# Hybrid decoder step on one core: head order of small products, per-pair recurrent decode outputs, and what each output projection pass waits for

## The chip, the cores and the metric

The kernel runs on one core of a Trainium2 chip. The metric is the device time of one execution in microseconds (us). A core has a matrix engine (PE, TensorE), three elementwise engines (DVE or VectorE, ACT or ScalarE, POOL or GpSimd), a queue that issues most transfers (SP), on-chip memory (SBUF), and the matrix engine's result memory (PSUM). Each engine runs its own instructions in a fixed order, so one that waits also holds up all that stand behind it on the same engine.

## The reference

One step of a decoder layer on 256 new prompt positions and 8 decode sequences with one new token each, 264 columns in all, in float32:

```
x = x + 0.5 * swiglu(rmsnorm(x), ffn1)
proj = rmsnorm(x) @ w_in                      # q, k, v and the recurrent columns
o_att  = windowed attention with sinks (16 query heads, 4 key/value heads)
o_rwkv = recurrent mixing (16 heads of 64), below
x = x + concat(o_att, o_rwkv) @ w_out
x = x + 0.5 * swiglu(rmsnorm(x), ffn2);  y = rmsnorm(x)
```

The recurrence, per head, with a 64x64 state S (value rows, key columns), is

```
sa = S @ (-kk)
S  = S * w + sa (x) (kk*a) + v (x) k        # w, a per key column; (x) is an outer product
y  = S @ r
out = (groupnorm(y) * ln_w + ln_b + sum(r*k*r_k) * v) * g
```

For the prompt it runs over 256 positions (done here in four chunks of 64). For decode it is a single step from a given state, for 8 sequences and 16 heads. The new states are outputs too. For one step the output can also be written without the new state, which is what the change uses: y = S0 @ (w*r) - (S0 @ kk) * (b.r) + v * (k.r), with b = kk*a and S0 the old state.

## The kernel before

Activations lie transposed: 128 features on the partitions, 264 columns (256 prompt positions, then 8 decode tokens). Every large product is split in two float32r parts: the weights arrive by SP in chunks of up to 128x512 (`raw`), ACT rounds them (`hi`), DVE subtracts (`lo`), and PE does three products for each 128x128 block (`gemm`, L125). These products write `acc` tiles, of which there are three; all other products write `m` tiles, of which there are five.

The step has four parts: the first feed-forward, the mixing, the output projection (with the mixing in one function, `mixing_body`), and the second feed-forward. In the mixing, 38 tiles of w_in are multiplied one after the other (`win`, L329). The rest of the mixing is written as Python generators in a list `tasks`; after each weight chunk `tick` (L76) advances every task by one step, so that small work is emitted between pieces of the large products. The order on each engine is then fixed when the program is built, by a scheduler that places the emitted instructions in a simulated timeline; the code's order and the blocks under high priority are only its input.

The tasks are: `prep` (L356), one for each pair of recurrent heads (8 pairs), which makes the decays, keys and the Gram matrices of the pair; `chain` (L470), one for each batch of two pairs (4 batches), which solves the triangular systems on DVE through DRAM scratch and carries the state over the chunks; `attend` (L713), one for each of eight query tiles of two heads; `dec_attend` (L754), decode attention; and `dec_rwkv` (L635), the decode recurrence of all pairs in sixteen slices of the state, on DVE and POOL. Each slice loads its piece of S (`ld<-in_st`), makes sa with a product on POOL and a sum on DVE (L656), updates S, stores it (`out_wkvs`, L663), and makes y with another product and sum (`yr`, L665). `dec_out` (L669) then transposes y, norms it and adds the affine terms (`yd`).

`XD` collects the eight decode columns of kk, decay, b, v, k and r; `XR` is its transposed copy. Loads of tasks share a ring `ld` of six buffers (L296). Query tiles `q` have a ring of three (L844), so the eviction of a fourth waits until the first attention task has used its own.

The output projection (L872) runs in three passes over the 16 input tiles: tiles 0 to 5 (recurrent pairs 0 to 5), tiles 8 to 15 (attention), tiles 6 and 7 (recurrent pairs 6 and 7). Ahead of each pass `need` (L863) lists the tasks that it drains; before the first pass it also drains `dec_rwkv` and `dec_out`. `drain` (L81) advances all tasks until those listed are done. `split` (L855) then rounds the inputs in two parts, for recurrent tiles after putting the decode columns `yd*gdec` in.

Two heads of a pair lie on partitions 0 to 63 and 64 to 127, `HALF[h]`. Products of 64 rows for one head use one half of the PE rows. Most loops over such products run all of head 0, then all of head 1 (L420, L442, L516, L528, L542, L553, L720); some already alternate (L448, L584).

Of the kernel before, what the change touches and what calls it, by code (L numbers as in the profile page):

```python
# [45 lines left out]
def body(tc, I, O):  # L46
# [34 lines left out]
    def drain(only):  # L81
        while any(g in only for g in tasks):
            tick()
# [9 lines left out]
    with ExitStack() as ctx:  # L93
# [195 lines left out]
        def mixing_body(mx, n2, n3):  # L289
# [14 lines left out]
            XD = fix((P, 6, NPAIR, NB), "XD")  # L304
            gdec = fix((P, NPAIR, NB), "gdec")
            bvdec = fix((P, NPAIR, NB), "bvdec")
# [12 lines left out]
            XR = fix((P, 6, 64), "XR")  # L319
            yr = fix((P, 64), "yr")  # L320
            sa = fix((P, 64), "sa")
            yd = fix((P, 64), "yd")
# [33 lines left out]
            def prep(p, bt, k, xrr, xk, xv):  # L356
# [61 lines left out]
                G.tensor_copy(bvdec[:, p, :], bv[:, NP:T])  # L418
                yield
                for h in range(2):  # L420
                    r = HALF[h]
                    gp = mp()
                    for c in range(4):
                        mm(gp[:, c * P:(c + 1) * P], BK[r, c, h:h + 2, :], KR[r, 0:2, c, :])
                    gm = ring((P, 4, P), "gm", NGM)
                    bt.Gm[k][h] = gm
                    tt(V, gm, gp.rearrange("p (c t) -> p c t", c=4), bc(msk.unsqueeze(1), (P, 4, P)), ALU.mult)
# [14 lines left out]
                for h in range(2):  # L442
                    r, o = HALF[h], HALF[1 - h]
                    for c in range(4):
                        mm(gv[r, c * 64:c * 64 + 64], bt.Gm[k][h][o, c, 0:64], bt.UV[o, c, k, r])
# [24 lines left out]
            def chain(bt):  # L470
# [45 lines left out]
                for h in range(2):  # L516
                    for k in range(n):
                        for c in range(4):
# [9 lines left out]
                for h in range(2):  # L528
                    r = slice(h * 64 + 32, h * 64 + 64)
                    for j in range(4 * n):  # L530
                        mm(ps[h * 64:h * 64 + 32, j * 32:j * 32 + 32], zs[r, j, :], TT[r, j, 32:64])
# [9 lines left out]
                for k in range(n):  # L541
                    for h in range(2):  # L542
                        r = HALF[h]
                        for c in range(4):
# [8 lines left out]
                for k in range(n):  # L553
                    for h in range(2):
                        r = HALF[h]
                        for c in range(1, 4):
                            x = (c - 1) * P
                            mm(pbs[k][r, x:x + 64], W[r, k, c - 1, :], bt.BT[k][c // 2][r, c % 2, r])
                            mm(pbs[k][r, x + 64:x + P], W[r, k, c - 1, :], bt.Gm[k][h][r, c, 64:128])
# [40 lines left out]
                for k in range(n):  # L600
                    A.copy(Ys[k][:, :NP], pY[:, k * NP:(k + 1) * NP])
                for k in range(n):
# [3 lines left out]
                gs = [gnorm(Ys[k][:, :NP], NP, Ys[k][:, :NP]) for k in range(n)]  # L606
# [4 lines left out]
                for k in range(n):  # L611
# [3 lines left out]
                    stt(o[:, :NP], o[:, :NP], vc(VLW + p), bt.bv[k][:, :NP], ALU.mult, ALU.add)  # L615
                    stt(o[:, :NP], o[:, :NP], vc(VLB + p), gp[:, :NP], ALU.add, ALU.mult)
                    A.copy(gdec[:, p, :], gp[:, NP:T])
# [3 lines left out]
            def gnorm(y, n, outp):  # L621
                yp = mp()
                mm(yp[:, :n], cm, y)
                sq = tmp()
                act(sq[:, :n], yp[:, :n], AF.Square)
                yield from pause(PW[3])
                vp = mp()
                mm(vp[:, :n], bo, sq[:, :n])
                r = tmp()
                act(r[:, :n], vp[:, :n], AF.Sqrt, scale=1.0 / 64, bias=eps[:, 1:2])  # L630
                V.reciprocal(r[:, :n], r[:, :n])  # L631
                tt(V, outp, yp[:, :n], r[:, :n], ALU.mult)
                yield

            def dec_rwkv(last):  # L635
                while last.left:
                    yield
                ps = mp()
                for i in range(6):
# [3 lines left out]
                A.copy(XR, ps[:, :384].rearrange("p (c t) -> p c t", c=6))  # L643
# [7 lines left out]
                for k in range(64 // n):  # L651
# [3 lines left out]
                    tt(G, t1, S, bj(0), ALU.mult)  # L655
                    V.tensor_reduce(out=sa[:, r], in_=t1, op=ALU.add, axis=AX.X)  # L656
# [6 lines left out]
                    SP.dma_start(O["wkvs"][:, r, :], S)  # L663
                    tt(G, t2, S, bj(5), ALU.mult)
                    V.tensor_reduce(out=yr[:, r], in_=t2, op=ALU.add, axis=AX.X)  # L665
                    if k % 2:
                        yield

            def dec_out():  # L669
                ps = mp()  # L670
                for h in range(2):
                    r = HALF[h]
                    mm(ps[r, 0:64], yr[r, :], ident[r, r])
                A.copy(yd, ps[:, 0:64])
                yield
                yield from gnorm(yd, 64, yd)
# [342 lines left out]
```

## Time and profile before

| | us |
|---|---|
| median of 3 runs | 2114.09 |
| lowest and highest | 2106.59, 2114.15 |
| the profiled execution | 2113.38 |
| its span, first to last instruction | 2111.5 |

The profile is of the one profiled execution. PE, DVE, ACT and POOL are the engines, and PEld is the weight load of PE, which overlaps it. L and a number is a line of the kernel; a helper that emits every operation has one line for all (L72 is every product, L56 most elementwise operations on two tensors), so groups are read by the names of tiles: `acc<-s,hi` is a product that reads tiles `s` and `hi` and writes `acc`. A float32 product is recorded as two MATMULs (two passes), a float32r product as one. In a group, `x` is the count of records, then busy time and mean duration, then the idle time just before them and who ended it. PEclk is the TensorE clock that was granted, as a share of full speed. In a view by windows each row is a stretch of the span, with the busy time and count of each engine, the clock, the share of DMA time and GB/s.

### The profile page before, as it was taken

The page shows a single profiled execution, that of the slowest core. Times are in us where ns is not written, and L with a number is a line of the kernel's source. Part 1 is how long each engine was busy: PE and PEld are TensorE (multiplying, and loading weights), DVE is VectorE, ACT ScalarE, POOL GpSimd, SP SyncE. Part 2 cuts the span into 40 slices and gives each one's busy share as a digit, 9 for nine tenths or more (in the row PEclk, how much of TensorE's full clock was granted, in tenths as well). Part 3 has the DMA queues.
Part 4 walks back from the last instruction along what each step waited for, and adds up shares of the span by engine and source line. Part 5 has one row for each costly group of instructions (what it writes and reads, how often), then busy time and mean ns, then how long its engine had stood idle before and what let it go on. Part 6 is the DMA issues. An engine that isn't in the chain of part 4 may idle for free.

```text
span 2111.5 us, 45349 instructions
## 1 busy us (share of the span) xinstructions
PE 2045.6 (97%) x16966; PEld 1997.4 (95%) x16966; DVE 1327.7 (63%) x2631; ACT 1061.5 (50%) x2078; POOL 311.1 (15%) x404
## 2 busy tenths in 40 slices
PE   8999999999999999999986899999999999999997
PEld 8999999999999999999975589899999999999997
DVE  5765555556555577876888646756555565655555
ACT  5644444444444576756532444644444444444445
POOL 0301011020101122201044110210110101011012
PEclk9999999999999999999996679999999999999998
DMA  6555565656555574544442155556555565555554
GB/s 221 176 175 187 175 206 170 211 181 181 182 177 185 178 233 150 150 118 129 122 139 79 38 147 183 165 181 181 181 178 184 177 185 182 178 184 175 187 177 139
DMA packets 227535, 356.29 MB, mean 169 GB/s; under 512 B 42177, under 2 KB 83153, under 8 KB 227281
## 3 DMA queue, kind: packets, MB, share of 16 engines
q1 hardware_dynamic: 221616, 344.72, 52.4%
q10 hardware_dynamic: 5696, 8.66, 1.1%
q8 instruction: 133, 2.18, 0.4%
q14 instruction: 90, 0.73, 0.1%
HBM read 345.15 MB, written 10.21 MB: 168 GB/s over the span
## 4 chain that ended last, share of the span: by engine, by line
PE 92%; DVE 4%; DMA 1%; ACT 1%; issue 1%; SPq 0%; DVEq 0%; ACTq 0%
PE acc L72 83%; PE m L72 9%; DVE lo L56 1%; DMA sb<-Xt 0%; DVE ld L56 0%; DMA raw<-in_gu 0%; DVE t L56 0%; DVE st L56 0%; ACT L66 0%; DVE y L56 0%; DVE t L631 0%; DVE s L59 0%; ACT t L66 0%; PE m L737 0%; DVE Xt L56 0%
## 5 line engine op out<-in xcount | busy, mean ns | idle before, releaser
L72 PE MATMUL acc<-s,hi 128*128 128x264 f32 x7072 | 1315.1, 286 | 13.3 <-ACT hi L121 7.7
L56 DVE TENSOR_TENSOR lo<-raw,hi 128x512 fp32r<-128x512 f32 (+2 forms) x1304 | 876.6, 676 | 606.4 <-ACT hi L121 583.2
L121 ACT CAST hi<-raw 128x512 fp32r<-128x512 f32 (+2 forms) x1304 | 780.4, 602 | 879.8 <-PE acc L72 802.2
L72 PEld LDWEIGHTS acc<-s,hi 128*128 128x128 f32 x7072 | 1107.0, 190 | 21.4 <-ACT hi L121 7.7
L72 PE MATMUL acc<-s,lo 128*128 128x264 f32 x3536 | 1013.4, 287 | 2.0 <-DVE lo L56 1.9
L72 PEld LDWEIGHTS acc<-s,lo 128*128 128x128 f32 x3536 | 669.1, 189 | 5.4 <-DVE lo L56 3.9
L72 PE MATMUL acc<-t,hi 128*128 128x264 f32 x2752 | 503.0, 285 | 1.6 <-ACT t L250 1.6
L72 PEld LDWEIGHTS acc<-t,hi 128*128 128x128 f32 x2752 | 426.5, 189 | 1.9 <-ACT t L250 1.8
L72 PE MATMUL acc<-t,lo 128*128 128x264 f32 x1376 | 388.8, 285 | 0.0
L56 POOL TENSOR_TENSOR t<-t,t 128x264 f32<-128x264 f32 (+1 forms) x146 | 156.8, 1074 | 1197.3 <-ACT hi L121 897.5
L72 PEld LDWEIGHTS acc<-t,lo 128*128 128x128 f32 x1376 | 258.4, 188 | 0.0
L56 DVE TENSOR_TENSOR t<-acc,t 128x264 f32<-128x264 f32 x164 | 70.9, 432 | 36.9 <-PE acc L72 36.5
L56 POOL TENSOR_TENSOR s<-s,s 128x264 f32<-128x264 f32 (+1 forms) x56 | 48.7, 871 | 199.0 <-ACT s L66 180.3
L66 ACT ACT_TABLE_LOAD x42 | 53.9, 1283 | 2.9 <-PEq L1011 1.2
L59 DVE SCALAR_TENSOR_TENSOR s<-acc,s 128x264 f32<-128x264 f32 x96 | 40.6, 427 | 16.6 <-PE acc L72 16.1
L59 DVE SCALAR_TENSOR_TENSOR x<-acc,x 128x264 f32<-128x264 f32 x96 | 40.6, 427 | 10.0 <-PE acc L72 9.5
L66 ACT ACTIVATE t<-t 128x264 f32<-128x264 f32 x94 | 40.0, 425 | 3.4 <-DVE t L56 1.9
L250 ACT CAST t<-t 128x264 fp32r<-128x264 f32 x86 | 35.5, 412 | 3.6 <-POOL t L56 2.1
L56 DVE TENSOR_TENSOR st<-X,Xt 128x60 f32<-128x60 f32 (+10 forms) x120 | 28.1, 234 | 12.9 <-DMA Xt<-sa 6.6
L342 POOL COPY shc<-pj 128x9 f32<-128x9 f32 x26 | 20.0, 768 | 85.9 <-DVE pj L56 85.9
L72 PE MATMUL m<-s,hi 128*128 128x264 f32 x160 | 30.3, 289 | 0.3 <-ACT hi L121 0.3
L66 ACT ACTIVATE t<-t,sta 128x256 f32<-128x256 f32 (+2 forms) x33 | 14.7, 446 | 28.3 <-DVE sta L63 27.1
(210 smaller groups left out, 1095.9 us busy)
## 6 DMA issues: line engine op xcount, KB each, us to landing
raw<-in_gu SPq DMA_DIRECT2D x688, 256.0 KB, 3.2
raw<-in_dn SPq DMA_DIRECT2D x224, 256.0 KB, 2.7
raw<-in_win SPq DMA_DIRECT2D x152, 256.0 KB, 3.3
raw<-in_dn SPq DMA_DIRECT2D x160, 192.0 KB, 2.7
raw<-in_wout SPq DMA_DIRECT2D x48, 256.0 KB, 3.0
raw<-in_wout SPq DMA_DIRECT2D x32, 128.0 KB, 2.4
xsp<-x ACTq DMA_DIRECT2D x16, 132.0 KB, 3.5
s<-xsp SPq DMA_DIRECT2D x16, 132.0 KB, 3.0
```

The lines of the kernel that those rows point to most:

```text
L56: return e.tensor_tensor(out=out, in0=a, in1=b, op=op)
L59: return V.scalar_tensor_tensor(out=out, in0=a, scalar=s, in1=b, op0=op0, op1=op1)
L66: return A.activation(out=out, in_=in_, func=f, **k)
L72: TE.matmul(out, lhsT, rhs, start=start, stop=stop, **k)
L121: A.copy(hi[:, :w], raw[:, :w])
L250: A.copy(hi, u)
L342: G.tensor_copy(shc[:, t, :], pj[:, NP:NP + NB + 1])
```

## The change

Five things:

1. Loops over products of half height take the two heads in turn, in `prep` (Gram matrices and the product `gv`), in `chain` (four loops) and in `attend`. For the Gram matrices and the attention scores both heads' PSUM tiles are taken at once.
2. `prep` computes the decode output of its pair. It loads the pair's old state, transposed (`sT`, a new input layout of the same values, two loads of 128x256), and multiplies it on PE with the eight tokens' kk and w*r: sixteen products of 64x64 by 2 columns, and one of 128x128 by 16 columns that sums b.r and k.r over each head. One ACT copy and three small DVE operations finish y, in `XD[:, 7]`.
3. `chain` copies these eight columns beside its 256 prompt columns, and the group norm (`gnorm`) and the affine terms run on 264 columns. `dec_out`, `bvdec`, `gdec`, `yd`, `yr` and `sa` go.
4. `dec_rwkv` becomes `dec_state`: it only updates the states, with sa taken from `XD[:, 0]`. Of its former operations for each slice the two sums on DVE and two of the four products on POOL go. It is spawned when the first projection pass begins, and drained after the last.
5. Before a pass that uses no attention tile, `drain` holds the attention tasks back; `split` is emitted at high priority.

```diff
-    def tick():
+    def tick(hold=()):
         for g in list(tasks):
-            if next(g, tasks) is tasks:
+            if g not in hold and next(g, tasks) is tasks:
                 tasks.remove(g)
...
-                for i, src in ((0, kk), (2, b), (3, xv), (4, kx), (5, xrr)):
+                for i, src in ((6, kk), (2, b), (3, xv), (4, kx), (5, xrr)):
                     G.tensor_copy(XD[:, i, p, :], src[:, NP:T])
+                dq = ring((P, 2, NB), "dq", 3)
+                tt(G, XD[:, 7, p, :], XD[:, 1, p, :], XD[:, 5, p, :], ALU.mult)
+                tt(G, dq, XD[:, 2:5:2, p, :], bc(XD[:, 5:6, p, :], (P, 2, NB)), ALU.mult)
+                st = [load(I["sT"][p, :, 4 * i:4 * i + 4], (P, 4, 64)) for i in range(2)]
...
-                G.tensor_copy(bvdec[:, p, :], bv[:, NP:T])
-                yield
-                for h in range(2):
-                    r = HALF[h]
-                    gp = mp()
-                    for c in range(4):
-                        mm(gp[:, c * P:(c + 1) * P], BK[r, c, h:h + 2, :], KR[r, 0:2, c, :])
+                dps = mp()
+                for i in range(NB):
+                    for h in range(2):
+                        r = HALF[h]
+                        mm(dps[r, 2 * i:2 * i + 2], st[i // 4][r, i % 4, :], XD[r, 6:8, p, i])
+                mm(dps[:, 16:32], bo, dq.rearrange("p s b -> p (s b)"))
+                dv = dps[:, 0:16].rearrange("p (b s) -> p s b", s=2)
+                A.copy(XD[:, 0, p, :], dv[:, 0])
+                tt(V, dq, dps[:, 16:32].rearrange("p (s b) -> p s b", s=2), XD[:, 0:4:3, p, :], ALU.mult)
+                tt(V, dq[:, 0], dv[:, 1], dq[:, 0], ALU.subtract)
+                tt(V, XD[:, 7, p, :], dq[:, 0], dq[:, 1], ALU.add)
+                yield
+                gps = [mp(), mp()]
+                for c in range(4):
+                    for h in range(2):
+                        r = HALF[h]
+                        mm(gps[h][:, c * P:(c + 1) * P], BK[r, c, h:h + 2, :], KR[r, 0:2, c, :])
...
                 for k in range(n):
-                    for h in range(2):
-                        r = HALF[h]
-                        for c in range(4):
+                    for c in range(4):
+                        for h in range(2):
+                            r = HALF[h]
                             mm(wus[k][r, c * P:c * P + P], TT[r, k * 4 + c, :], bt.KR[k][r, 0:3:2, c, :])
...
                     A.copy(Ys[k][:, :NP], pY[:, k * NP:(k + 1) * NP])
+                    A.copy(Ys[k][:, NP:T], XD[:, 7, bt.p0 + k, :])
...
                     S = load(I["st"][:, r, :], shp)
                     t1, t2 = tmp(shp), tmp(shp)
-                    tt(G, t1, S, bj(0), ALU.mult)
-                    V.tensor_reduce(out=sa[:, r], in_=t1, op=ALU.add, axis=AX.X)
+                    tt(G, t1, bc(XR[:, 3, r].unsqueeze(2), shp), bj(4), ALU.mult)
                     tt(V, S, S, bj(1), ALU.mult)
-                    yield
-                    tt(V, t2, bc(sa[:, r].unsqueeze(2), shp), bj(2), ALU.mult)
+                    tt(V, t2, bc(XR[:, 0, r].unsqueeze(2), shp), bj(2), ALU.mult)
                     tt(V, S, S, t2, ALU.subtract)
-                    tt(G, t1, bc(XR[:, 3, r].unsqueeze(2), shp), bj(4), ALU.mult)
                     tt(G, S, S, t1, ALU.add)
                     SP.dma_start(O["wkvs"][:, r, :], S)
-                    tt(G, t2, S, bj(5), ALU.mult)
-                    V.tensor_reduce(out=yr[:, r], in_=t2, op=ALU.add, axis=AX.X)
-                    if k % 2:
-                        yield
+                    yield
...
                 for h in range(2):
                     r = HALF[h]
+                    mm(spp[h][:, 0:256], q[r, P:NP], kT[p][r, 0:NP])
+                for h in range(2):
+                    r = HALF[h]
+                    mm(spp[h][:, 256:384], q[r, 0:P], kT[p][r, 0:P])
...
-                drain(need(ks))
-                for k in ks:
-                    split(k)
+                drain(need(ks), att if max(ks) < 8 else ())
+                if pi == 0:
+                    dst = spawn(dec_state())
+                with tc.high_priority():
+                    for k in ks:
+                        split(k)
...
+            drain([dst])
             return xr
```

More of the change, by code (lines that the diff above doesn't have):

```diff
@@ L515, in chain @@
                 ps = mp()
-                for h in range(2):
-                    for k in range(n):
-                        for c in range(4):
+                for k in range(n):
+                    for c in range(4):
+                        for h in range(2):
                             j = k * 4 + c
@@ L527, in chain @@
                 ps = mp()
-                for h in range(2):
-                    r = slice(h * 64 + 32, h * 64 + 64)
-                    for j in range(4 * n):
+                for j in range(4 * n):
+                    for h in range(2):
+                        r = slice(h * 64 + 32, h * 64 + 64)
                         mm(ps[h * 64:h * 64 + 32, j * 32:j * 32 + 32], zs[r, j, :], TT[r, j, 32:64])
@@ L541, in chain @@
                 for k in range(n):
-                    for h in range(2):
-                        r = HALF[h]
-                        for c in range(4):
+                    for c in range(4):
+                        for h in range(2):
+                            r = HALF[h]
                             mm(wus[k][r, c * P:c * P + P], TT[r, k * 4 + c, :], bt.KR[k][r, 0:3:2, c, :])
@@ L553, in chain @@
                 for k in range(n):
[L554 to L557, printed above, removed]
+                    for c in range(1, 4):
+                        x = (c - 1) * P
+                        for h in range(2):
+                            r = HALF[h]
                             mm(pbs[k][r, x:x + 64], W[r, k, c - 1, :], bt.BT[k][c // 2][r, c % 2, r])
+                        for h in range(2):
+                            r = HALF[h]
                             mm(pbs[k][r, x + 64:x + P], W[r, k, c - 1, :], bt.Gm[k][h][r, c, 64:128])
@@ L605, in chain @@
                 gps = []
-                gs = [gnorm(Ys[k][:, :NP], NP, Ys[k][:, :NP]) for k in range(n)]
+                gs = [gnorm(Ys[k]) for k in range(n)]
                 for _ in range(PW[3] + 1):
```

76 lines of the change are left out of this document (26 added, 50 removed).

## The prediction

> **What bounds the kernel now.** I read the page first: the span, the granted clock, the chain that ended last.
>
> ```profile
> span 2111.5 us, 45349 instructions
> ...
> PEclk9999999999999999999996679999999999999998
> ...
> PE 92%; DVE 4%; DMA 1%; ACT 1%; issue 1%; SPq 0%; DVEq 0%; ACTq 0%
> ```
>
> The chain runs on PE nearly everywhere. Only slices 22 to 24 of 40 have a lower clock: the end of the mixing. The changed program leaves both feed-forwards in their order, so I cut the mixing and the projection into stages by the view of windows. A (790 to 1048) is most of the w_in tiles with the pairs; B ends where the sixth query tile is evicted; C ends at the first product of the projection; D is its three passes. Two short windows of C and the first pass of D follow.
>
> ```profile
> core 0: us, PE busy (x) PEld busy (x) DVE busy (x) ACT busy (x) POOL busy (x), PEclk, DMA share, GB/s
> 790.00:1048.00 258.00, 256.71 (x2379) 242.09 (x2379) 196.12 (x508) 167.60 (x383) 42.21 (x90) 0.99 0.47 134
> 1048.00:1154.00 106.00, 79.38 (x752) 71.18 (x752) 88.41 (x246) 35.05 (x91) 41.85 (x55) 0.83 0.41 117
> 1154.00:1231.00 77.00, 65.80 (x375) 47.27 (x374) 48.73 (x169) 31.83 (x101) 16.22 (x31) 0.59 0.21 63
> 1231.00:1330.00 99.00, 98.70 (x844) 96.56 (x845) 60.41 (x125) 45.90 (x96) 7.29 (x15) 0.97 0.52 162
> ```
> ```profile
> 1160.00:1170.00 10.00, 10.00 (x74) 8.50 (x73) 3.99 (x10) 1.49 (x5) 2.14 (x3) 0.50 0.08 26
> 1210.00:1220.00 10.00, 10.00 (x33) 6.54 (x33) 4.41 (x22) 4.92 (x21) 0.00 (x0) 0.50 0.61 173
> 1231.00:1266.00 35.00, 34.70 (x320) 32.56 (x321) 16.05 (x42) 13.92 (x32) 2.54 (x10) 0.92 0.51 148
> ```
>
> A and D are PE from end to end. In B PE idles 26.6 us while DVE works 88.4 of 106. In C PE works 65.8 of 77, at a clock of 0.59, on attention and the last batch, with no large product beside it. What PE waited for in B and C, from the view of waits:
>
> ```profile
> PE m L72 <- DVE TN L513: 10.8, 1, 10.8
> PE m L737 <- DVE t L63: 9.4, 3, 7.5
> PE m L72 <- ACT s L601: 4.9, 1, 4.9
> PE m L72 <- ACT t L66: 3.7, 2, 2.1
> PE acc L72 <- DVE q L59: 3.6, 1, 3.6
> ```
>
> The three that end on DVE make 23.8 us. DVE's groups in B say what it did; these five are the decode recurrence, 12 of its 16 slices:
>
> ```profile
> L56 DVE TENSOR_TENSOR ld<-ld,t 128x256 f32<-128x256 f32 x12 | 6.6, 548 | 0.0
> L56 DVE TENSOR_TENSOR ld<-ld,XR 128x256 f32<-128x256 f32 x12 | 6.3, 523 | 0.0
> L56 DVE TENSOR_TENSOR t<-sa,XR 128x256 f32<-128x256 f32 x12 | 6.0, 496 | 0.0
> L656 DVE TENSOR_REDUCE sa<-t 128x4 f32<-128x256 f32 x12 | 4.9, 409 | 3.4 <-POOL t L56 3.4
> L665 DVE TENSOR_REDUCE yr<-t 128x4 f32<-128x256 f32 x12 | 4.9, 408 | 0.0
> ```
>
> Together 28.7 us of B.
>
> **The change, part by part. Stage A: price of the small products.** From the timeline of PE (start, duration, count of records, two to a product):
>
> ```profile
> 949.93 1.10 PE L72 MATMUL m<-C,bk 64*128 64x64 f32 x8
> 1052.87 1.71 PE L72 MATMUL m<-kr,bk 64*128 64x128 f32 x16
> 1057.00 0.96 PE L72 MATMUL m<-uv,gm 64*64 64x64 f32 x16
> 1057.90 1.11 PE L72 MATMUL m<-C,bk 64*128 64x64 f32 x16
> 1058.93 0.92 PE L72 MATMUL m<-C,XD 64*64 64x64 f32 x24
> 1067.81 2.56 PE L72 MATMUL m<-kr,TT 64*64 64x128 f32 x32
> ```
>
> The first row is four products of one head in a row (the scheduler had parted the heads there), the fourth is eight in alternation: the same time for twice the work. So alternation halves this form. C,XD alternates already and takes 38 ns a record; uv,gm, of its size in head order, takes 60.
> - Gram matrices (kr,bk), halved: 1.71 to 0.86 us, 7 pairs in A: -6.0. Ends: -6.0 and 0.
> - gv (uv,gm) at 38 ns: 0.96 to 0.61 us, 7 pairs: -2.5.
> - W and U (kr,TT), halved: 1.28 us off each batch, two in A: -2.6.
> - The two 32x32 loops and the one behind W I leave at nothing.
> - Added: 16 products of 64x64 by 2 columns, 32 records. The trace has no product so narrow. Nearest is C,XD, the same weights with 64 columns, alternating: 38 ns, 1.2 us; the far end is kr,TT in head order, 80 ns, 2.6 us. I take 1.2, and 0.1 for the product by 16 columns: 7 times 1.3, +9.1.
> - PE now also waits for a POOL product and two loads, with the Gram matrices and the w_in products queued behind. In the changed instruction order these products stand behind the one of r*k, to which every pair already comes, and some 80 to 130 large products behind the pair's start; I price the wait at nothing. SP issues sixteen loads more, 0.34 us each by the store's row below, where DMA works 0.47 of A. The three short DVE operations, the ACT copies and the wider norm ride on engines that are idle 62 and 90 us of A.
>
> A: -2. Ends: -11 (added products at nothing) and +19 (at 80 ns, alternation worth nothing).
>
> **Stage B.** The five DVE groups go from here: 88.4 - 28.7 is 60, with under 1 added. The order shows it too: DVE has 188 instructions from the third query eviction to the last, formerly 282. PE's 79.4 us at a clock of 0.83 are 66 at full speed; pair 8 and batch 2 bring that to 65 by the prices above. So PE bounds B at 65 if all waits go. The longest, for the last solve (TN), should go: in the new order its first consumer stands 147 large products after the first attention scores, 17 us at D's 844 records in 98.7 us, more than the 10.8. I let 8 of 26.6 us of waits stay: 73, -33. Ends: -41 (65), and -15 (91: PE stays at 0.83 and TN's wait remains).
>
> **Stage C.** PE's groups in C:
>
> ```profile
> L72 PE MATMUL m<-t,s 128*64 128x256 f32 x28 | 11.9, 624 | 0.0
> L72 PE MATMUL m<-s,q 64*128 64x256 f32 x20 | 11.0, 647 | 0.0
> L72 PE MATMUL m<-kr,TT 64*64 64x128 f32 x32 | 7.3, 421 | 0.4 <-ACT TT L534 0.4
> L72 PE MATMUL m<-t,s 128*64 128x128 f32 x26 | 6.6, 400 | 0.3 <-DVE t L742 0.3
> L72 PE MATMUL m<-s,q 64*128 64x128 f32 x20 | 5.6, 373 | 0.0
> L72 PE MATMUL m<-qd,ld 64*128 64x4 f32 x16 | 1.9, 354 | 0.0
> L72 PE MATMUL m<-t,C 128*128 128x64 f32 x2 | 0.7, 450 | 0.0
> L72 PE MATMUL m<-yd,C 128*128 128x64 f32 x2 | 0.7, 448 | 0.0
> ```
>
> - Scores (s,q): 16.6 us for ten heads; four of five pairs alternate in the new order: halved, -6.6.
> - kr,TT halved: -3.6. The norm of yd (1.4) goes; transposing XR, 12 products before B ended, comes to 10 here, +0.9.
> - The changed order starts the first pass earlier by little: 14 of 16 heads have their output products before it, formerly 15, and 8 of the decode scores no longer precede it. The hold hardly acts: six attention tasks are already emitted by then. One head's t,s (18.5 us over 14, 1.3) and qd,ld (1.9) move on: -3.2.
>
> PE's 65.8 becomes 52. The 11.2 us of waits stay, since the steps of a softmax from engine to engine remain; 63, -14. Ends: 0 (these steps pace C) and -20.
>
> **Stage D.** The 3.2 us moved here cost about half at full clock: +2. The state update lies beside the passes now: by the three rows of B, 16 times 1.57 is 25 us of DVE, which is idle 38.6 of D and 19 of the first pass. Its POOL work, and what it puts on SP:
>
> ```profile
> L56 POOL TENSOR_TENSOR ld<-ld,t 128x256 f32<-128x256 f32 x16 | 12.6, 787 | 40.9 <-issue 21.2 <-DVE ld L56 16.0 <-PE m L72 2.0
> SPq L663 <- POOL ld L56: 28.5, 14, 6.4
> L663 SPq DMA_DIRECT2D out_wkvs<-ld x16: 343/343/383, 1068.0 to 1187.2; - x16
> ld<-in_st SPq DMA_DIRECT2D x16, 128.0 KB, 2.3
> ```
>
> POOL's two products, 1.6 us a slice, are covered (7.3 busy of 99). On SP each store waits for POOL with weight chunks queued behind it: 28.5 us in 14 waits before, when nothing urgent lay behind. Six raw buffers and four of hi and lo cover about four chunks. If that cover is gone, PE waits for `lo`. I add 4 us: D is +6. Ends: 0 and +28.
>
> **Sum.** -2 -33 -14 +6 is -43. The profiled execution took 2113.38, its span and 1.9 around it, 0.03% below the median of 2114.09: 2070.
>
> **A rule that speaks against it.** The Trainium skill, TensorEngine Tiling (Array Packing), section Restrictions and Gotchas, says that different row tiles cannot access the same PSUM bank at once. Scores and Gram matrices have a bank for each head; gv, kr,TT and the new decode products put both heads in one. C,XD does so too and takes 38 ns, not 60, so the trace does not bear the rule out in full. By it the sum would be the first rival's.
>
> **Rivals.**
> 1. Halves that share a bank do not overlap. Then gv and kr,TT gain nothing and the new products cost 2.7 us a pair: A rises by 14.7, B by 3, C by 3.6: 2091. For it: gv's 60 ns. Against: C,XD's 38. 0.13.
> 2. The attention chain, with three query buffers, paces B and C, not DVE: B -15, C 0, A and D as above: 2102. For it: waits on ACT and on L63. Against: DVE's 88.4 of 106. 0.12.
> 3. C runs at full clock, as work is denser: 52 times 0.59 is 31, with 11 of waits 42: 2049. Against: the windows at 1160 and 1210, PE busy all 10 us at 0.50. The Trainium skill, TensorE: Matmul & The Clock Gate, Part 1, has the clock return after some 3.4 us of sustained work; those windows do not agree. 0.09.
> 4. Slower: the state update holds up the first passes. If the chunk behind each slice waits for its load (2.3), two DVE steps (1.0), POOL (0.8) and the store's issue (0.34), 4.4 us for 16 slices is 71 in place of D's 4: 2137. It decides from 3.4 us a slice (43 plus half a per cent, 10.6, over 16). Against: SP's waits averaged 2.0. 0.07.
>
> **How the numbers follow.** My forecast has the remaining 0.59, with its own range of 2052 to 2086. 2047 to 2100 takes in rival 1, most of 3 and half of 2. Half a per cent is about what a measurement tells from no change: faster is all but rival 4 and the upper part of rival 2, 0.88; same 0.05; slower 0.07.
>
> **What would show it.** Right: decode products at 40 ns a record or less; kr,bk near 0.9 us; the 10.8 us wait for TN gone; DVE no longer full in B; the first projection product some 49 us earlier; the passes at about 105 us. Wrong: PE waiting for `lo` in the first pass, or for loads of sT in a pair; C as long as before; records of the new products at 80 ns.

## The result and the profile after

The changed kernel takes 2088.59 us (median of 4 runs, 2087.01 to 2091.04) where the kernel before, run beside it, takes 2113.88 (2106.59 to 2114.15): a ratio of 0.9893, 95% interval 0.9874 to 0.9911. That is 25 us less; the forecast was 43 less, 2070, with 2047 to 2100 as its range. The profiled execution took 2087.01 us. From the page of the changed kernel, the span, the granted clock in 40 slices and the chain of work that ended last:

```profile
span 2085.0 us, 45855 instructions
...
PEclk9999999999999999989999889999999999999999
...
PE 89%; DVE 4%; DMA 3%; ACT 1%; issue 1%; SPq 0%; POOL 0%; DVEq 0%; ACTq 0%; POOLq 0%
```

The hole of 6, 6, 7 in the clock at the end of the mixing has shrunk to 8, 8, and a new 8 stands in slice 18. DMA has three times its former share of the chain.

The stages have moved, so I cut them here at events that both kernels have: A runs from the first eviction of a shifted tile (`pj`, DVE) to the first query eviction, B to the sixth query eviction, C to the first product of the projection. D is cut in three: from there to the sixteenth residual add (first pass), to the seventeenth (the gap ahead of the second pass), and to the 48th. All are starts of rows in the timelines of DVE and PE, rounded to 0.1 us before they are subtracted.

| us | A | B | C | D first pass | D gap | D rest | all |
|---|---|---|---|---|---|---|---|
| before | 268.2 | 106.6 | 76.9 | 47.0 | 2.5 | 63.1 | 564.3 |
| after | 280.2 | 70.1 | 49.3 | 66.9 | 9.6 | 61.1 | 537.2 |
| difference | +12.0 | -36.5 | -27.6 | +19.9 | +7.1 | -2.0 | -27.1 |
| forecast | -2 | -33 | -14 | +6 for all of D | | | -43 |

The view by windows of the changed kernel, with the borders of this table, A from 790 on (columns as in the prediction), and the kernel before in its D:

```profile
core 0: us, PE busy (x) PEld busy (x) DVE busy (x) ACT busy (x) POOL busy (x), PEclk, DMA share, GB/s
790.00:1060.00 270.00, 260.29 (x2601) 242.69 (x2601) 201.21 (x534) 167.70 (x388) 42.72 (x98) 0.97 0.46 134
1060.00:1130.00 70.00, 68.47 (x766) 62.30 (x766) 53.10 (x177) 33.79 (x86) 1.91 (x5) 1.00 0.47 135
1130.00:1179.00 49.00, 34.20 (x379) 23.93 (x379) 36.79 (x152) 28.86 (x96) 4.85 (x9) 0.89 0.29 82
1179.00:1317.00 138.00, 122.44 (x935) 114.63 (x936) 97.46 (x201) 59.42 (x133) 40.85 (x56) 0.89 0.52 165
```
```profile
1231.00:1343.00 112.00, 108.80 (x905) 104.62 (x906) 73.41 (x151) 56.67 (x124) 14.95 (x24) 0.98 0.52 163
```

B is what was forecast: DVE is busy 53 of 70 us, PE is full and at full clock. A was full before and now has 10 us in which PE stands. C gave twice what was forecast: its clock is 0.89, not 0.59. D lost its full PE: 15.6 us idle, and 0.89 of the clock where the kernel before had 0.98. Who ended PE's waits, over mixing and projection (us in total, times, longest), and the same for the passes alone:

```profile
PE acc L72 <- DVE lo L56: 6.3, 8, 1.4
PE m L732 <- DVE t L63: 5.8, 5, 1.9
PE acc L72 <- ACT s L851: 5.3, 2, 3.7
PE m L72 <- DVE gm L56: 5.2, 1, 5.2
PE m L72 <- ACT t L66: 3.7, 1, 3.7
PE m L72 <- DMA ld<-in_cv: 2.8, 3, 1.8
PE acc L72 <- POOL s L56: 2.6, 1, 2.6
PE m L72 <- DMA ld<-in_kc: 2.5, 4, 1.4
```
```profile
PE acc L72 <- ACT s L851: 5.3, 2, 3.7
PE m L72 <- DMA ld<-in_cv: 2.8, 3, 1.8
PE m L732 <- DVE t L63: 2.7, 2, 1.9
PE acc L72 <- POOL s L56: 2.6, 1, 2.6
PE m L72 <- DMA ld<-in_kc: 2.5, 4, 1.4
...
PE acc L72 <- DVE lo L56: 1.1, 2, 0.6
```

The 10.8 us for TN are gone. In the passes PE hardly waits for `lo`, which I had feared. It waits for the inputs of the passes (`s` of L851 and of POOL are the split tiles; 3.7 us of that lie at the end of C), for the caches of decode attention, and for a softmax. In A there is one wait of 5.2 us, for a Gram matrix. Between the two windows of D, 12 of the 26 us more are idle time of PE (15.6 against 3.2) and 14 are longer busy time, at the lower clock.

### The profile page after: what moved, and what is told of

It is laid out like the page before. It is cut to its first block, busy times and chain, and to the rows that moved or that the text cites. A ratio compares the mean times of both kernels' runs of the same rounds, so it can differ in the third digit from the quotient of the medians.

```text
span 2085.0 us, 45855 instructions
## 1 busy us (share of the span) xinstructions
PE 2019.5 (97%) x17226; PEld 1974.6 (95%) x17226; DVE 1308.6 (63%) x2618; ACT 1059.0 (51%) x2081; POOL 286.8 (14%) x372
## 4 chain that ended last, share of the span: by engine, by line
PE 89%; DVE 4%; DMA 3%; ACT 1%; issue 1%; SPq 0%; POOL 0%; DVEq 0%; ACTq 0%; POOLq 0%
PE acc L72 82%; PE m L72 7%; DMA raw<-in_gu 1%; DVE lo L56 1%; ACT t L66 1%; DMA out_wkvs<-ld 0%; DMA ld<-in_st 0%; DMA sb<-Xt 0%; DMA TT<-sb 0%; ACT L66 0%; DVE t L723 0%; DVE t L56 0%; DVE y L56 0%; DVE s L59 0%; DVE t L63 0%
## 5 line engine op out<-in xcount | busy, mean ns | idle before, releaser
L56 DVE TENSOR_TENSOR t<-acc,t 128x264 f32<-128x264 f32 x164 | 70.9, 432 | 36.1 <-PE acc L72 35.9
L56 POOL TENSOR_TENSOR s<-s,s 128x264 f32<-128x264 f32 (+1 forms) x56 | 48.8, 875 | 188.4 <-ACT s L66 171.7
L399 POOL COPY XD<-t 128x8 f32<-128x8 f32 x40 | 16.1, 402 | 117.8 <-DVE t L59 106.1
```

What stands on the lines that cost most here:

```text
L56: return e.tensor_tensor(out=out, in0=a, in1=b, op=op)
```

## The experiments

Times are medians; ratios are against runs of the kernel before on the same chip. There it took 2113.1 us beside e1 to e4, 2115.0 beside e5 to e8 and 2116.0 beside e9 to e11, so a few us between rows of different groups say little. The same stages for all runs (profiled executions):

| | us | ratio, interval | A | B | C | D first | D gap | D rest |
|---|---|---|---|---|---|---|---|---|
| before | 2113.9 | | 268.2 | 106.6 | 76.9 | 47.0 | 2.5 | 63.1 |
| after | 2088.6 | 0.9893 (0.9874 to 0.9911) | 280.2 | 70.1 | 49.3 | 66.9 | 9.6 | 61.1 |
| e1 heads in order | 2097.8 | 0.9927 (0.9904 to 0.9950) | 282.6 | 73.4 | 53.8 | 66.7 | 9.8 | 62.4 |
| e2 heads alone | 2101.4 | 0.9941 (0.9917 to 0.9964) | 261.1 | 106.9 | 64.3 | 54.3 | 2.5 | 63.0 |
| e3 update second | 2082.3 | 0.9855 (0.9831 to 0.9879) | 282.6 | 70.9 | 46.7 | 51.9 | 10.2 | 69.5 |
| e4 waits as before | 2098.8 | 0.9927 (0.9900 to 0.9954) | 281.5 | 95.6 | 52.7 | 54.1 | 2.5 | 62.4 |
| e5 no pair products | 2082.8 | 0.9858 (0.9830 to 0.9886) | 262.8 | 77.6 | 49.1 | 69.8 | 10.8 | 61.3 |
| e6 solve later | 2096.2 | 0.9921 (0.9896 to 0.9946) | 283.3 | 72.2 | 48.8 | 67.0 | 10.5 | 61.2 |
| e7 no update | 2066.5 | 0.9780 (0.9753 to 0.9806) | 278.3 | 67.1 | 47.2 | 51.4 | 1.9 | 62.4 |
| e8 = e3 and e6 | 2089.5 | 0.9893 (0.9869 to 0.9917) | 284.5 | 74.3 | 46.0 | 51.6 | 10.2 | 69.6 |
| e9 other ring | 2081.7 | 0.9848 (0.9831 to 0.9865) | 280.9 | 69.7 | 47.2 | 66.9 | 4.9 | 59.5 |
| e10 update in FFN 2 | 2071.3 | 0.9794 (0.9779 to 0.9810) | 281.6 | 71.3 | 46.7 | 53.3 | 1.9 | 62.1 |
| e11 gv in two banks | 2088.8 | 0.9875 (0.9859 to 0.9891) | 277.5 | 71.9 | 48.5 | 66.6 | 10.6 | 61.1 |

### What the order of heads is worth: e1 and e2

The changed kernel with all seven loops back in head order, and the kernel before with the seven loops alone. For one loop of e1:

```diff
-                for c in range(4):
-                    for h in range(2):
-                        r, o = HALF[h], HALF[1 - h]
+                for h in range(2):
+                    r, o = HALF[h], HALF[1 - h]
+                    for c in range(4):
                         mm(gv[r, c * 64:c * 64 + 64], bt.Gm[k][h][o, c, 0:64], bt.UV[o, c, k, r])
```

> The changed kernel (2088.6) with all seven loops of part 1 back in the order of heads; everything else of the change stays. Theory A, alternation is worth what the records say: by the intervals of the two traces, Gram matrices 1.64 against 1.09 us a pair (8 pairs, 4.4), gv 0.28 a pair (2.2), kr,TT 0.6, the loops behind W 0.85 and the 32x32 loops 0.85 a batch (4 batches, 9), scores 334 against 163 ns a record (64 records, 11): 27 us in all, and all of it stands on PE's path: about 2115, no faster than the kernel before. Theory B, only what lies where PE has no waits counts: scores in the stage behind the sixth query tile are hidden by the softmax steps that pace it, 10 to 15 us: 2099 to 2103. Theory C, alternation is worth more than its records, because head order leaves PE at half clock in that stage as in the kernel before: over 2120, with the clock between the sixth query eviction and the first projection product at 0.6 instead of 0.86.

> The kernel before (2114) with part 1 alone: seven loops alternate, decode recurrence and waits as before. Theory A (parts add): 27 us less PE work, 2087. Theory B (each stage has its own bound): the stage with the pairs gains 10, the stage that DVE bounds (third to sixth query eviction) gains nothing and keeps its 10.8 us wait for TN, the stage behind it gains 5 to 13: 2091 to 2099. Theory C (the gain of the change comes from the decode recurrence leaving the path, alternation is swallowed by waits): 2104 or more.

Undoing the order costs 7 to 9 us, not 27: theory B in e1, a little less than its 10 to 15. Alone, alternation gives 12.5 us (0.59% of 2113): between B and C in e2. The records did shrink. The scores in the C of the changed kernel, by the view of groups:

```profile
L72 PE MATMUL m<-s,q 64*128 64x256 f32 x20 | 4.0, 485 | 0.0
L72 PE MATMUL m<-s,q 64*128 64x128 f32 x20 | 2.2, 300 | 0.0
```

The same rows of the kernel before had 11.0 and 5.6 us, in the prediction, for the most part at half clock. But a stage pays only what it is short of. In A, e2 gained 7 us, where PE hardly waits in the kernel before (1.2 us); in B it gained nothing, and the wait for TN was 12.9 us, as DVE was still full of the decode recurrence; in C it gained 12.6, of which the first pass behind it took 7.3 back (54.3 against 47.0). In the C of the changed kernel PE stands for 14.8 of 49 us, for steps of softmaxes, for a norm and for the first split, and undoing the order costs 4.5 us there, though PE's busy time goes from 34.2 to 46.1 of 49 and 54 us and the clock from 0.89 to 0.74. The window of C in e1:

```profile
1135.00:1189.00 54.00, 46.10 (x359) 33.22 (x358) 38.07 (x148) 25.25 (x89) 5.45 (x10) 0.74 0.28 80
```

### Where the gain of B and the loss of D come from: e4 and e3

e4 puts the narrower wait back: the state update starts with the last batch and is drained before the first pass.

```diff
                     if len(bat) == len(BATCH):
+                        dst = spawn(dec_state())
...
-                drain(need(ks), att if max(ks) < 8 else ())
-                if pi == 0:
-                    dst = spawn(dec_state())
-                with tc.high_priority():
-                    for k in ks:
-                        split(k)
+                if pi == 0:
+                    drain([dst])
+                drain(need(ks))
+                for k in ks:
+                    split(k)
...
-            drain([dst])
```

> The changed kernel without part 5 and without the late spawn of part 4: the state update starts with the last batch and is drained before the first pass, attention is not held, the splits have no high priority. Alternation and the decode outputs per pair stay. Theory A, what mattered is the decode recurrence's DVE work before the first pass: its 16 slices are now 3 products, 1.3 us, 20 us of DVE in all, where DVE works 78 of 102 us between the first query evictions and the sixth; they fit, the wait for TN stays away, and the first pass loses what it lost: 41 to 44 us from first to last add: about 2078, faster than the change. Theory B, the passes' narrower wait is worth what it costs: the stages before the first pass grow by 15 to 20, the passes fall by 15: 2086 to 2094. Theory C, the narrower wait is the change's gain: above 2100.

Theory A fell, though 20 us of DVE seemed to fit; 2098.8 lies between theories B and C. B is 95.6 us instead of 70.1, and the waits of the kernel before are back:

```profile
PE m L72 <- DVE TN L523: 9.2, 1, 9.2
...
PE acc L72 <- DVE q L59: 6.3, 1, 6.3
```

D falls by 18.6 from its 137.6 us at the same time. So with the update early, and the hold and the priorities undone in the same run, B pays 25 us and D saves 19. e3 has one line changed, the pass at which the update is spawned:

```diff
-                if pi == 0:
+                if pi == 1:
                     dst = spawn(dec_state())
```

> The changed kernel with the state update spawned at the second projection pass, not the first. Theory A, the state update (16 loads, 16 stores, 128 KB each, three DVE products a slice) is what makes the first pass 55 us long from its first to its last residual add, where the kernel before takes 41: the first pass falls to 43 to 46, the gap of 9.6 us before the second pass's first add closes to 4, the second pass (45 us from its first to its last add) grows by 5 at most: 2088.6 - 10 = 2078 to 2081. Theory B, decode attention and the late attention heads are what holds the first pass (PE waits 5.3 us for kc and cv, 2.7 for a softmax): the first pass stays over 51, and the time stays within 4 us of 2088 or rises, since the second pass now shares its transfers with the update.

Theory A in its direction, not in full: the first pass is 15 us shorter, but the gap stays at 10.2 and the rest of D grows by 8.4. The time is 6 us lower. The timeline of DVE in e3 at the start of the second pass (start, duration) and POOL's row beside it:

```profile
1233.05 0.84 DVE L56 TENSOR_TENSOR ld<-ld,XR 128x256 f32<-128x256 f32 x1
1233.81 0.83 DVE L56 TENSOR_TENSOR t<-XR 128x256 f32<-128x256 f32 x1
...
1239.84 0.83 DVE L56 TENSOR_TENSOR t<-XR 128x256 f32<-128x256 f32 x1
1240.59 0.42 DVE L56 TENSOR_TENSOR s<-acc,s 128x264 f32<-128x264 f32 x1
```
```profile
1232.81 9.84 POOL L56 TENSOR_TENSOR t<-XR 128x256 f32<-128x256 f32 x13 [3.79 <-ACT XR L655]
```
```profile
1241.16 0.78 PE L72 MATMUL acc<-s,hi 128*128 128x264 f32 x2 [2.70 <-DVE s L56]
```

Ten products of the update stand in a row on DVE, at 0.83 us each while POOL works on its own, and the residual add that frees an `acc` tile comes behind them.

### What the update costs in all, and by which way: e7, e9, e10

e7 leaves the slices out and copies the old states to the output.

```diff
                         A.dma_start(O["sh"], shc)
+                        A.dma_start(O["wkvs"], I["st"])
...
-                for k in range(64 // n):
...
```

> The changed kernel without the sixteen slices of the state update: the old states are copied to the output by one transfer on ACT's queue where the last pairs are, so the new decode states are left uncomputed. Theory A, the update is what the first pass pays for: from its first to its last residual add 41 to 46 us instead of 55, first add earlier by 6 as in the run with the update in the second pass, and the second pass 42 to 44: 2088.6 - 16 = 2072, some 10 below the run with the update in the second pass (2082.3), where the second pass took 8 more. Theory B, whatever is moved into the passes, decode attention's caches and the two late heads set them: the first pass over 50, the time over 2082.

Theory A, and more than it said: 22 us by the medians. D is 115.7 us, 22 less than in the changed kernel and 3 above the kernel before. e9 keeps the update in the first pass, and loads the slices to other buffers than those that the caches use.

```diff
-                    S = load(I["st"][:, r, :], shp)
+                    S = tmp(shp)
+                    SP.dma_start(S, I["st"][:, r, :])
```

> The changed kernel with the slices of the old state loaded into the large ring of temporaries (25 buffers) instead of the ring of six that the caches of decode attention, the bias tiles and g2 use too; the update stays in the first pass. The run without the update took 22 us less than the changed kernel: 6 at the start of the first pass, 11 in it, 8 in the gap behind it. Theory A, the shared ring is the cause: loads of kc and cv stand behind slices, so decode attention and with it the second pass come late: PE's waits for kc and cv (5.3 us) go, the first pass takes 46 to 49 us in place of 55, the gap before the second pass 2 to 4 in place of 9.6: about 2077. Theory B, it is the order on DVE and SP, and the transfers themselves (4 MB in and out beside the weights), whatever the ring: the first pass over 52, the time within 4 of 2088.

Both in part. The gap falls from 9.6 to 4.9 us, not quite to theory A's 2 to 4, and the waits for kc and cv from 5.3 to 2.4; the first pass doesn't fall at all, as theory B had it, and the rest of D falls by 1.6. So the shared ring held decode attention, and with it the second pass, 6 us back; the other 16 us of the update don't come from it. The view of groups shows something that the ring doesn't change and that may make them, though no run tests it alone: DVE stands at the head of a slice for its load, with weight halves and residual adds behind it in its order. The changed kernel, then e9:

```profile
L56 DVE TENSOR_TENSOR ld<-ld,XR 128x256 f32<-128x256 f32 x16 | 7.9, 504 | 17.0 <-DMA ld<-in_st 12.3 <-issue 3.3 <-PE m L72 1.4
```
```profile
L56 DVE TENSOR_TENSOR t<-t,XR 128x256 f32<-128x256 f32 x16 | 7.5, 489 | 11.3 <-DMA t<-in_st 11.2
```

e10 moves the slices into the second feed-forward, one for each hidden tile from the fourth on.

```diff
+        XR = cp.tile([P, 5, 64], F32, name="XR")
...
                         hs[j - f0] = (hi, lo)
+                    if bg and f > 2:
+                        dep[0] = u
+                        next(bg, None)
...
+                z = fp.tile([P, 1], F32, tag="dz", bufs=2, name=uid("dz"))
+                ts(G, z, dep[0][:, 0:1], 0.0, ALU.mult)
...
-                    tt(V, S, S, bj(1), ALU.mult)
+                stt(S, S, z, bj(1), ALU.add, ALU.mult)
...
-                ffn(n3, xr, I["gu2"], I["dn2"], nxt)
+                ffn(n3, xr, I["gu2"], I["dn2"], nxt, bg=states(fp))
```

> The changed kernel with the sixteen slices of the state update moved out of the projection into the second feed-forward, one to each hidden tile from the fourth on; the transposed XR stays where it is made, in a buffer that lives on. Each slice's first DVE product also adds a zero that POOL makes from a tile of that hidden tile, so that no slice runs earlier. There PE is full at full clock, DVE is busy 115 of 200 us, POOL 20 and DMA 0.58. Theory A, the update is free there: the time of the run without it, 2066, up to 2070 for the zero and the added transfers. Theory B, it costs there too, as in the second projection pass (8 us), since a store in SP's queue that waits for POOL holds weights back: 2074 to 2082, with PE waiting for lo or hi in the second feed-forward.

Theory A, a little above its upper end: 2071.27 us, 0.9794 of the kernel before (0.9779 to 0.9810), the best of all versions that compute everything, 17 us below the changed kernel (21 by the ratios). The windows of e10 (the passes, and all behind them) and of the changed kernel behind its passes:

```profile
1179.00:1297.00 118.00, 113.60 (x938) 107.20 (x939) 78.62 (x166) 59.83 (x137) 19.30 (x30) 1.00 0.56 168
1297.00:2066.00 769.00, 755.21 (x6184) 753.86 (x6183) 477.38 (x795) 370.00 (x662) 129.42 (x140) 0.99 0.61 183
```
```profile
1317.00:2085.00 768.00, 753.94 (x6186) 752.57 (x6186) 444.15 (x750) 371.70 (x663) 96.91 (x94) 0.99 0.57 178
```

The second feed-forward takes 33 us more of DVE and 32 of POOL, and grows by 1 to 2 us (e7, with no update in it, takes as long from its last residual add to its end, 770 us): the same work that costs 20 us in the passes is hidden here, where each slice has a hidden tile's time to itself and PE waits 0.5 us for DVE, in the changed kernel 0.4. The clock of the passes is 1.00.

### What stage A lost: e5 and e6

e5 leaves out the products of a pair's decode output and their loads; the four small operations on DVE and ACT stay.

```diff
-                st = [load(I["sT"][p, :, 4 * i:4 * i + 4], (P, 4, 64)) for i in range(2)]
...
-                dps = mp()
-                for i in range(NB):
...
-                mm(dps[:, 16:32], bo, dq.rearrange("p s b -> p (s b)"))
-                dv = dps[:, 0:16].rearrange("p (b s) -> p s b", s=2)
-                A.copy(XD[:, 0, p, :], dv[:, 0])
+                A.copy(XD[:, 0, p, :], XD[:, 6, p, :])
...
```

> The changed kernel without the sixteen decode products of a pair, the product that sums b.r and k.r, and the two loads of the transposed state; the three small DVE operations and the ACT copy stay, on other inputs. The decode columns of the recurrent part are therefore left uncomputed, and the state update uses a wrong sa. Theory A, the pair products cost what their records say: in the stage with the pairs (first shifted tile to first query eviction, 268 us before, 261 with alternation alone, 280 in the changed kernel) 7.2 for the narrow ones, 2.1 for the sum and 1.8 for the large product behind them: the stage falls to 269, the time to 2077. Theory B, they cost 19 (280 - 261), twice their records, through waits that they bring with them (gm 5.2 us, lo 4.3): the stage falls to 261 to 264, the time to 2070. Theory C, the waits come from the rest of the change: the stage stays above 274, the time above 2083.

A falls by 17 us, by theory B, to 262.8; but B grows by 7.5, and PE waits 8.2 us for DVE there, in the changed kernel 1.5. A and B together fall by 9.9, near the 11 of the records of these products in theory A. The time falls by less than either theory had it, by 6 us to theory C's border, since D is 4.3 us longer in this run. The timeline of PE of the changed kernel at the fourth pair (start, duration), and DVE's rows beside it:

```profile
900.16 1.10 PE L72 MATMUL m<-XD,ld 64*64 64x2 f32 x32
901.20 0.40 PE L72 MATMUL m<-dq,C 128*128 128x16 f32 x2
901.53 1.16 PE L72 MATMUL m<-kr,bk 64*128 64x128 f32 x16
...
911.05 0.47 PE L72 MATMUL m<-uv,gm 64*64 64x64 f32 x2 [5.18 <-DVE gm L56]
```
```profile
907.13 0.41 DVE L56 TENSOR_TENSOR TT<-TT,C 32x256 f32<-32x256 f32 x1 [4.38 <-DMA TT<-sb]
...
909.41 0.86 DVE L56 TENSOR_TENSOR TT<-TT,C 32x256 f32<-32x256 f32 x2 [1.15 <-DMA TT<-sb]
910.30 1.29 DVE L56 TENSOR_TENSOR gm<-m,C 128x512 f32<-128x512 f32 x2
```

The 32 narrow records take 1.04 us to the next start, 33 ns each. The longest wait is DVE's order: the first batch's solve comes back through a DRAM buffer, DVE stands for it 4.4 and 1.2 us, and the Gram evictions are behind. e6 puts that solve behind the next bk transposes, by a zero that depends on them:

```diff
+                    zero = fix((P, 1), "zero")
+                    ts(G, zero, bts[1].BT[1][1][:, 1, 127:128], 0.0, ALU.mult)
...
-                        tt(V, v, v, bc(ident[x:x + 32, x:x + 32].unsqueeze(1), (32, n * 4, 32)), ALU.add)
+                            stt(v, v, zero[x:x + 32, :], idb, ALU.add, ALU.add)
```

> The changed kernel with one order changed: the four additions of the unit diagonal to the first batch's solved triangles (TT, which come through a DRAM buffer) read a zero that POOL writes from the last bk transpose of the second batch, so that DVE takes them behind the Gram evictions and two weight halves. Theory A, the longest wait of the pair stage (PE for gm, 5.2 us, DVE standing 4.4 us at the first TT) and the half clock behind it (uv,gm and C,bk at 911 to 915 take twice their usual time, 3 us) come from this order: the stage falls from 280 to 272, the time to 2080. Theory B, the wait only moves (to lo behind TT, or to the product with TN): the stage stays over 277, the time over 2085.

> The state update spawned at the second pass together with the later first solve: the edits of the two runs of those names in one kernel. Theory A, they lie in different stages and add: 6.3 and 8 below the changed kernel, 2074 to 2076. Theory B, the solve's order gives nothing: 2081 to 2084.

Theory B, and worse: A doesn't shrink, the time is 6 to 8 us longer in e6, and in e8 7 longer than in e3. The wait for gm is gone, and PE waits for TN of that solve instead. A line of the waits of e6, and DVE's rows there:

```profile
PE m L72 <- DVE TN L533: 6.4, 1, 6.4
```
```profile
909.14 1.50 DVE L59 SCALAR_TENSOR_TENSOR TT<-TT,zero,C 32x256 f32<-32x256 f32 x3 [0.19 <-DMA TT<-sb]
919.37 0.19 DVE L56 TENSOR_TENSOR st<-X,Xt 128x30 f32<-128x30 f32 x1 [8.73 <-DMA ld<-in_sT]
919.48 0.89 DVE L533 STREAM_TRANSPOSE TN<-TT 32x256 f32<-32x256 f32 x2
```

The first batch's triangles are back in time now: DVE stands 0.19 us for them. Their transposes (TN) come 9 us later, behind the first step of the second batch's solve, for which DVE stands 8.7 us; its triangles come through DRAM too (the profile names a load of sT, which SP issued right behind theirs). So the wait moved, and it is still one of order: while DVE stands for one solve's way through DRAM, what lies behind it waits as well.

### Do halves that share a bank hinder each other: e11

```diff
-                gv = mp()
+                gvs = [mp(), mp()]
...
-                        mm(gv[r, c * 64:c * 64 + 64], bt.Gm[k][h][o, c, 0:64], bt.UV[o, c, k, r])
-                A.copy(KR[:, 2], gv[:, :256].rearrange("p (c t) -> p c t", c=4))
+                        mm(gvs[h][r, c * 64:c * 64 + 64], bt.Gm[k][h][o, c, 0:64], bt.UV[o, c, k, r])
+                for h in range(2):
+                    r = HALF[h]
+                    A.copy(KR[r, 2], gvs[h][r, :256].rearrange("p (c t) -> p c t", c=4))
```

> The changed kernel with gv, the product of uv and gm, written to a PSUM tile for each head, not both heads to one; two ACT copies of half height take the place of one. Theory A, halves that share a bank do not run side by side: then the sixteen records of a pair, 0.61 to 0.87 us in the changed kernel, take 0.3 to 0.45: 2 to 3 us over eight pairs, 2085 to 2087. Theory B, sharing a bank costs nothing: the records keep their time, and the total stays within what another order moves it, 2085 to 2092. The records decide, not the time.

Theory B. Sixteen records of gv in a row, both heads in one bank (changed kernel), then a bank for each (two pairs of e11):

```profile
849.94 0.68 PE L72 MATMUL m<-uv,gm 64*64 64x64 f32 x16
```
```profile
826.16 0.85 PE L72 MATMUL m<-uv,gm 64*64 64x64 f32 x16
...
880.99 0.69 PE L72 MATMUL m<-uv,gm 64*64 64x64 f32 x16
```

43 ns a record with one bank, 43 to 53 with two. The rule of the Trainium skill that the prediction weighed (TensorEngine Tiling (Array Packing), Restrictions and Gotchas) would have the two-bank form faster; the measurement doesn't agree.

## Why the prediction was right, and where not

The direction and the range held, and so did the main mechanism; 18 us of the forecast gain of 43 are missing. They are missing in stage D; the errors in A and C, of 14 us each, cancel by luck.

- **Stage B, right.** -33 forecast, -36.5 measured. DVE bound it with the decode recurrence: with the update back in this stage (e4) B is 95.6 us and TN's wait 9.2; with all of it out, 70.1 and PE full. That even the smaller update, three products a slice, holds B up by 25 us when it lies there was not foreseen.
- **Stage D, the step that failed: "I add 4 us" for the state update beside the passes.** It cost 20 to 22 us of D: 137.6 against 115.7 without it (e7) and 117.3 with it in the second feed-forward (e10). That e10's 2071.3 us is so near the sum's 2070 is luck, since A and C are off there too. I had looked for the price at PE's wait for `lo`, which stayed small (1.1 us in the passes). What happened instead: the loads of the slices shared a ring of six with the caches of decode attention, which put the second pass 6 us back (e9); slices stood in DVE's order for their loads (12.3 us) with residual adds and splits behind, which is seen in the rows but not priced by a run of its own; PE, idle 15.6 us in pieces, fell to a clock of 0.89. My rival 4 had the right place, with 4.4 us a slice and a condition of 3.4 (3.6, as the sum already has 4 us); it came to 1.4 us a slice, so it took back half the gain and didn't turn the sign.
- **Stage A, two terms mis-sized:** -2 forecast, +12 measured. Alternation alone gave 7 us in A (e2) where the sum had 11: the Gram records of a pair take 1.16 us, not 0.86. The new products cost 17 us in A (e5) where the sum had 9. Their records came out as priced (about 1.4 us a pair), and no wait for their loads or for POOL came, as "I price the wait at nothing" had it. But other waits grew, which the sum didn't have: 5.2 us for a Gram matrix, with half the clock behind it, and 4.3 for `lo`, where e5 has 3.4 for TN and 1.4 for `lo`. B gave 7.5 of the 17 back. In e1 head order costs only 2.4 us in A, but e1 doesn't have the wait for the Gram matrix, so that difference is not the price of the order alone.
- **Stage C, mis-sized the other way:** -14 forecast, -27.6 measured. I left the clock at 0.59; it rose to 0.89, which is most of rival 3 (42 us for C; 49.3 measured). Alternation gives 4.5 (e1) to 12.6 (e2) of it; from e2 (64.3) to e4 (52.7) the decode outputs' leaving gives 11.6, and the late update with the hold the last 3.4. The waits in C rose from 11 to 15 us. What sets the clock there is not settled.
- **The rivals.** 1 (shared banks): its 2091 is near the result by chance; the narrow records take 33 ns and e11 gains nothing. 2 (query ring paces B): no, PE is full in B. 3: half right, above. 4: right place, a third of its price, and not by its way, weights held on SP: PE's wait for `lo` is 1.1 us.
- **What would show it.** Narrow products under 40 ns: yes. kr,bk near 0.9 us: no, 1.16. TN's wait gone: yes. DVE no longer full in B: yes. First projection product 49 us earlier: 51.4. Passes at about 105 us: no; that sum took D to end at 1330, 13 us ahead of the last residual add, so the like figure is 119, and it came to 137.6. PE waiting for loads of sT: no such wait.

## What to carry to other kernels

Off the critical engine is not free: work that is moved to run beside a stage can cost what it delays in the order of its own engine, where the stage has urgent rows of its own (residual adds, splits). Look for the longest stage that is bound by another engine and hardly waits for this one (here the second feed-forward, DVE 0.58 busy), and put the work there one piece at a time, held back by a data dependence if the scheduler would pull it forward. When small products become faster, first ask in which stage they end last; the same edit gave 7, 0 and 13 us in three stages, and 7 of the 13 were lost again in the next.

## What the runs showed of the hardware

- DVE's 128x256 products took 0.41 to 0.42 us alone and 0.83 while POOL ran products back to back (rows of e3 above: POOL's thirteen in 9.84 us are 0.76 each, DVE starts one each 0.75). The Trainium skill (SBUF — State Buffer, Who interferes with whom) says that a DVE instruction with two SBUF inputs contends with a POOL instruction that reads SBUF; the trace agrees. The residual add in the same stretch has one input in PSUM, and took 0.42 us while POOL ran.
- After the wait of 5.2 us in A the clock stayed at half for 11 us in which PE had work throughout; windows of the changed kernel:

```profile
911.00:915.00 4.00, 3.95 (x33) 3.48 (x33) 2.74 (x5) 0.68 (x3) 0.00 (x0) 0.50 0.26 51
915.00:920.00 5.00, 5.00 (x46) 4.01 (x46) 0.49 (x1) 4.17 (x12) 0.19 (x1) 0.50 0.78 199
920.00:922.00 2.00, 2.00 (x11) 2.00 (x11) 0.00 (x0) 1.19 (x3) 0.00 (x0) 0.50 0.48 94
922.00:924.00 2.00, 2.00 (x17) 1.82 (x15) 1.06 (x6) 0.62 (x1) 0.00 (x0) 0.94 0.01 4
```

The Trainium skill (TensorE: Matmul & The Clock Gate, Part 1) has full clock back after some 3.4 us of sustained work. Here it took three times that, for the most part on small products. Half of the 11 us, about 5, is an estimate of what that cost. But A is only 2 us shorter in e7, where PE has no wait over 1.6 us in A, so the price of such a wait in a whole stage isn't shown.
